# Output projections of two branches moved in between the pieces of a local attention group

## Chip, cores and metric

One Trainium2 chip, one of its cores. The time is the device time of one execution in microseconds; the kernel before has a median of 2757.5 us over 3 runs (2754.83 to 2759.94).

## What is computed

One decoder layer over 2048 tokens of width 1024, all in float32. Cut to what matters:

```python
h = x * (1 + scale) + shift
q, k, v, g_attn, u, B, C, g_conv, m_attn, m_conv = split(h @ W_in)
# A: three groups of 4 heads (dilation 1, 4, 16), each query sees 129 keys at its stride
o = sum_g(softmax_weight_g * attention_g(q, k, v))        # (2048, 512)
a_out = (o * silu(g_attn)) @ W_attn_out                   # 512 -> 1024
# B: gated short convolution
s_out = (B * conv3(C * u) * silu(g_conv)) @ W_conv_out    # 1024 -> 1024
merged = sigmoid(m_attn) * a_out + sigmoid(m_conv) * s_out
x = LayerNorm(alpha * x + (1 + gate) * (merged @ W_o))
```

## The kernel before, in words

Every float32 product is made of three products of float32r parts: each operand is split into a high part (a cast on ScalarE) and a low part (a subtraction on VectorE; the helper `split`, L465 to L467), and `mm3` (L563) or `pass3` (L119) adds high-high, high-low and low-high in PSUM. The instructions of all splits thus carry the lines L466 and L467.

The tile framework sets semaphores and the order of each engine's queue: it goes by the order of the program, lets ready instructions pass those that wait, and waits where a tile's buffer is not free. All loads and stores are issued by SyncE on one queue. Four stages follow one another.

1. The big projection h @ W_in, without v (L720 to L902). It works on blocks: `step` (L635) loads two 128-column blocks of weights, makes seven combinations of their quarters (`stationary_parts`, L536), and `products` (L578) forms seven block products over four rows of prepared `T` blocks, a Strassen-Winograd form with seven products in place of eight. Preparing one row of `T` (`t_row`, L513) takes seven splits and four subtractions, each of 128x512. `step` puts its products into the list `todo`, and they are traced in the next call, after the next weights have been prepared (`flush`, L621). Results go to DRAM scratch (q and k to `qk_scr`, the convolution branch to `y_scr`, the gates to `sg_scr` and `ga_scr`). During the first half `bias_tiles` (L704) turns the relative bias into tiles: it loads rows of `lagd` as overlapping windows, flips them with a product by `flip` (L714), copies and stores them. It is called for three groups, each right after a `step`, so before that step's products in program order.

2. Attention (`attention_stage`, L54). A list of segments `segs` holds the v products of 512-token quarters (pieces); `run_segs` (L94) walks it, loads weights up to 4 segments ahead, splits them up to 2 ahead, and runs pieces of attention hung behind the segments by `after`: scores and exponentials (`qk`), transposes (`tr`), weighted values (`pv`). First come the groups with dilation 4 and 16 for all quarters, called the dilated groups below, then the group with dilation 1, the local group (L352 to L418). Behind the local group's heads of each quarter `done` (L358) works out the softmax weights of the three groups through DRAM, and `merge` (L394) sums the three outputs and stores them in `om_scr`. The tile `o0` of each head has one buffer.

3. The output projections of the branches (L957 to L971). `co(0)`, then the attention branch over both halves, then `co(1)`: `step` and `products` again, over rows of `y_scr` (`load_y`) and `om_scr` (`load_o`). `gated` (L927) adds the last two block terms from PSUM (L940), multiplies by the gate (L941), and on the second branch adds the first one's result from `pa_scr` on GpSimd (L943). The sum goes to `mg_scr`, in blocks of 128 tokens.

4. The last projection and the norm (L974 to L1032). `load_w` scales the rows of W_o by the gate (L989); 8 steps over pairs of 128-token blocks from `mg_scr`; `norm` adds the residual (L1008, L1009), takes mean and variance with `bn_stats` and `bn_aggr` on VectorE (L1012 to L1016), scales on ScalarE (L1021), multiplies by g (L1022), adds b on GpSimd (L1023) and stores. `products_by_row` (L603) exists and is used for the first step of stage 1 alone: it runs all seven products of one row before the next row, with seven banks open.

```python
todo.append(lambda ...: (how or products)(S_, T, rows, *consumer()))   # L642, in step
```

## Time and profile before

| | |
|---|---|
| median of 3 runs | 2757.5 us |
| the profiled execution | 2760.77 us, span 2759.0 us, mean granted clock 0.944 |
| PE busy | 2478.2 us (90%) |
| DVE busy | 1821.2 us (66%) |
| ACT busy | 1059.2 us (38%) |
| POOL busy | 117.2 us (4%) |
| DMA | 364.03 MB, mean 132 GB/s |

PE is TensorE, DVE VectorE, ACT ScalarE, POOL GpSimd, SP SyncE. Busy time is a mean over the stages above. A granted clock of 1.00 is TensorE at 2.4 GHz, 0.50 at 1.2 GHz. The DMA share is the mean busy share of 16 DMA engines. Times in the rows are microseconds from the start of the span.

### The profile page before, as it was taken

Reading aid. Unit: us, or ns where it says so; the run is one execution under the profiler, and the core shown is the slowest. Engines: PE = TensorE matmul, PEld = TensorE weight load, DVE = VectorE, ACT = ScalarE, POOL = GpSimd, SP = SyncE. Lnnn points to the kernel's source line nnn. Section 1 sums busy time; section 2 is a strip of 40 time slices with the busy share of each in tenths; the row PEclk is TensorE's granted clock in tenths of the full one; section 3 lists DMA queues with packets and bytes.
Section 4 is the critical chain, followed back from the end, with each engine's and each line's share of the span. In section 5 each row is a group of like instructions: output and inputs, shape, how many; then the busy total and the mean of one; then the engine's idle time right before and its main releaser. Section 6 shows DMA issues by size and latency. Waiting matters only on the chain.

```text
span 2759.0 us, 31825 instructions
## 1 busy us (share of the span) xinstructions
PE 2478.2 (90%) x11734; PEld 2086.0 (76%) x11734; DVE 1821.2 (66%) x2996; ACT 1059.2 (38%) x1763; POOL 117.2 (4%) x78
## 2 busy tenths in 40 slices
PE   4998999999999999999999799999997358978886
PEld 2776788888877888888888599999986336656665
DVE  8753467667667555676655345544788787777987
ACT  5322333333344223333333355554653223243432
POOL 2000000000000000000000000000000000203123
PEclk8999999999999999999999899999998578989998
DMA  6333322213353333222222444534566655667343
GB/s 235 124 102 101 112 86 69 69 63 106 122 171 119 100 115 110 73 70 69 69 99 92 157 134 134 168 115 137 159 202 196 189 173 186 230 230 231 113 145 103
DMA packets 192265, 364.03 MB, mean 132 GB/s; under 512 B 20925, under 2 KB 91756, under 8 KB 192108
## 3 DMA queue, kind: packets, MB, share of 16 engines
q1 hardware_dynamic: 192108, 361.99, 40.7%
q8 instruction: 92, 1.51, 0.2%
q14 instruction: 65, 0.53, 0.1%
HBM read 268.03 MB, written 93.90 MB: 131 GB/s over the span
## 4 chain that ended last, share of the span: by engine, by line
PE 70%; DVE 11%; DMA 8%; issue 5%; ACT 3%; POOL 1%; SPq 1%; POOLq 0%; DVEq 0%; ACTq 0%
PE pb L566 19%; PE pb L567 19%; PE pb L568 19%; PE mm L123 3%; PE mm L121 3%; PE mm L122 3%; DVE tl L467 2%; DMA og<-o_scr 1%; PE pt L203 1%; DMA xs<-in_xn 1%; DMA ab<-al_scr 1%; DVE w2l L467 1%; DVE ab L407 1%; DMA raw<-mg_scr 1%; DVE o L408 0%
## 5 line engine op out<-in xcount | busy, mean ns | idle before, releaser
L566 PE MATMUL pb<-th,w2h 128*128 128x512 f32 x2304 | 918.6, 402 | 98.9 <-ACT th L466 74.0
L567 PE MATMUL pb<-tl,w2h 128*128 128x512 f32 x2304 | 916.2, 399 | 45.4 <-DVE tl L467 45.3
L568 PE MATMUL pb<-th,w2l 128*128 128x512 f32 x2304 | 907.9, 397 | 2.6 <-DVE w2l L467 2.6
L566 PEld LDWEIGHTS pb<-th,w2h 128*128 128x128 f32 x2304 | 441.8, 192 | 223.4 <-ACT th L466 96.0
L567 PEld LDWEIGHTS pb<-tl,w2h 128*128 128x128 f32 x2304 | 442.9, 192 | 148.3 <-DVE tl L467 57.4
L568 PEld LDWEIGHTS pb<-th,w2l 128*128 128x128 f32 x2304 | 442.9, 192 | 96.8 <-DVE w2l L467 4.9
L467 DVE TENSOR_TENSOR w2l<-raw,w2h 128x1024 fp32r<-128x1024 f32 (+1 forms) x192 | 237.8, 1239 | 166.2 <-ACT w2h L466 166.0
L466 ACT CAST w2h<-raw 128x1024 fp32r<-128x1024 f32 (+1 forms) x192 | 198.7, 1035 | 363.3 <-PE pb L567 348.4
L575 ACT COPY t<-pb 128x512 f32<-128x512 f32 x298 | 173.8, 584 | 412.8 <-PE pb L568 373.9
L121 PE MATMUL mm<-whi,hhi 128*128 128x256 f32 x768 | 253.4, 331 | 28.5 <-ACT hhi L466 28.4
L123 PE MATMUL mm<-whi,hlo 128*128 128x256 f32 x768 | 249.3, 327 | 3.4 <-DVE hlo L467 2.8
L122 PE MATMUL mm<-wlo,hhi 128*128 128x256 f32 x768 | 249.6, 326 | 1.9 <-DVE wlo L467 1.9
L121 PEld LDWEIGHTS mm<-whi,hhi 128*128 128x128 f32 x768 | 185.8, 242 | 32.2 <-ACT hhi L466 32.1
L123 PEld LDWEIGHTS mm<-whi,hlo 128*128 128x128 f32 x768 | 184.7, 242 | 5.5 <-DVE hlo L467 5.4
L122 PEld LDWEIGHTS mm<-wlo,hhi 128*128 128x128 f32 x768 | 186.1, 243 | 2.4 <-DVE wlo L467 2.3
L566 PE MATMUL pb<-th,w1h 128*128 128x512 f32 x384 | 154.2, 402 | 18.1 <-DVE big L1008 10.1
L466 ACT CAST w2h<-xs 128x1024 fp32r<-128x1024 f32 (+1 forms) x96 | 99.5, 1037 | 167.0 <-PE pb L567 141.1
L567 PE MATMUL pb<-tl,w1h 128*128 128x512 f32 x384 | 152.2, 396 | 0.0
L568 PE MATMUL pb<-th,w1l 128*128 128x512 f32 x384 | 151.8, 395 | 0.0
L943 POOL TENSOR_TENSOR big<-big,t 128x512 f32<-128x512 f32 x32 | 47.7, 1498 | 2437.2 <-DMA t<-pa_scr 2390.2
L466 ACT CAST w1h<-t 128x512 fp32r<-128x512 f32 (+1 forms) x96 | 58.8, 613 | 170.5 <-PE pb L567 163.1
L467 DVE TENSOR_TENSOR w2l<-xs,w2h 128x1024 fp32r<-128x1024 f32 (+1 forms) x96 | 116.1, 1210 | 11.5 <-ACT w2h L466 8.4
(161 smaller groups left out, 3072.7 us busy)
## 6 DMA issues: line engine op xcount, KB each, us to landing
raw<-in_w_main SPq DMA_DIRECT2D x152, 512.0 KB
qk_scr<-big SPq DMA_DIRECT2D x48, 512.0 KB
raw<-in_w_v SPq DMA_DIRECT2D x48, 512.0 KB
sg_scr<-big SPq DMA_DIRECT2D x32, 512.0 KB
big<-sg_scr SPq DMA_DIRECT2D x32, 512.0 KB
qr<-qk_scr SPq DMA_DIRECT2D x48, 256.0 KB
ab<-al_scr SPq DMA_DIRECT2D x48, 256.0 KB
kr<-qk_scr SPq DMA_DIRECT2D x36, 256.0 KB
```

The lines of the kernel that those rows point to most:

```text
L121: PE.matmul(o, a[0], b[0], start=start, stop=False)
L122: PE.matmul(o, a[0], b[1], start=False, stop=False)
L123: PE.matmul(o, a[1], b[0], start=False, stop=stop)
L203: PE.transpose(ps[:, n * P:(n + 1) * P], P_t[b][:, a:a + P], ident)
L407: V.tensor_mul(av, av, og)
L466: S.copy(hi, src)
L467: V.tensor_sub(lo, src, hi.bitcast(F32))
L566: PE.matmul(bank, a[0], b[0], start=start, stop=False, **kw)
L567: PE.matmul(bank, a[0], b[1], start=False, stop=False, **kw)
L568: PE.matmul(bank, a[1], b[0], start=False, stop=stop, **kw)
L575: S.copy(r, bank)
L943: G.tensor_add(o, o, a_)
```

## The change

Stage 3 is gone. In the attention stage each quarter of the local group is followed by 8 segments that project that quarter of the convolution branch (`co_segs`), and by 8 that project the quarter before of the attention branch (`ao_segs`); the last quarter's `ao_segs` come at the end. They are plain products with `pass3`, 24 (co) or 12 (ao) of 128x512 for each 128 output columns, gated by one multiplication from PSUM; the ao ones add co's result on VectorE. To make room, several tiles have fewer buffers. `bias_tiles` issues its loads at once and puts its flip products behind the step's products. The last projection's first step goes by rows, and its mean and variance come from two ScalarE passes with accumulated sums.

```diff
-        raw = wp.tile([P, DM], F32, name="raw", bufs=3)
+        raw = wp.tile([P, DM], F32, name="raw", bufs=2)
...
+    def parts_of(xs, store):
+        hi = hp.tile([P, CH], F32R, name="hhi", bufs=13)
+        lo = hp.tile([P, CH], F32R, name="hlo", bufs=13)
+        split(hi, lo, xs)
+        store.append((hi, lo))
...
-                hi = hp.tile([P, CH], F32R, name="hhi", bufs=9)
-                lo = hp.tile([P, CH], F32R, name="hlo", bufs=9)
...
+    def prep_rows(srcs, store):
+        def pre():
+            for src in srcs:
+                xs = hp.tile([P, CH], F32, name="xs", bufs=3)
+                SP.dma_start(xs, src)
+                parts_of(xs, store)
         return pre
...
+    def gemm(unit, rhs, base=0):
+        ps = bank("mm", 3)
+        for k, xk in enumerate(rhs):
+            sl = slice((base + k) * P, (base + k + 1) * P)
+            pass3(ps, [t[:, sl] for t in unit], xk, k == 0, k == len(rhs) - 1)
+        return ps
...
-        qr = kq.tile([P, CH], F32, name="qr", bufs=2)
-        kr = kq.tile([P, P + CH], F32, name="kr", bufs=2)
+        qr = kq.tile([P, CH], F32, name="qr", bufs=1)
+        kr = kq.tile([P, P + CH], F32, name="kr", bufs=1)
...
-                    pt = pa.tile([P, 256], F32, name="p", bufs=10)
+                    pt = pa.tile([P, 256], F32, name="p", bufs=8)
...
-                t = whole("ptf", transposed([(b, b) for b in range(4)]), slice(0, CH), 2)
+                t = whole("ptf", transposed([(b, b) for b in range(4)]), slice(0, CH), 1)
...
-            va = pa.tile([P, 3, 256], F32R, name="va", bufs=4)
-            vb = pa.tile([P, 3, 256], F32R, name="vb", bufs=4) if g < 2 else None
+            va = pa.tile([P, 3, 256], F32R, name="va", bufs=3)
+            vb = pa.tile([P, 3, 256], F32R, name="vb", bufs=3) if g < 2 else None
...
+    def co_segs(c):
+
+        ys, at = [], slice((c % 2) * CH, (c % 2 + 1) * CH)
+        for d in range(KT):
+            def coseg(i, unit, d=d):
+                sg = pm.tile([P, CH], F32, name="sg", bufs=2)
+                SP.dma_start(sg, sg_scr[c // 2, 1, d, :, at])
+                V.tensor_mul(sg, sg, gemm(unit, ys))
+                SP.dma_start(pa_scr[c // 2, d, :, at], sg)
+            seg([w_co[d]], coseg, prep_rows([y_scr[c // 2, k, :, at] for k in range(KT)], ys) if d == 0 else None)
+
+    def ao_segs(c):
+
+        os_, at, box = [], slice((c % 2) * CH, (c % 2 + 1) * CH), {}
+        for d in range(KT):
+            def aoseg(i, *units, d=d):
+                if units:
+                    box["u"] = units[0]
+                sg = pm.tile([P, CH], F32, name="sg", bufs=2)
+                co = pm.tile([P, CH], F32, name="co", bufs=2)
+                SP.dma_start(sg, sg_scr[c // 2, 0, d, :, at])
+                SP.dma_start(co, pa_scr[c // 2, d, :, at])
+                V.tensor_mul(sg, sg, gemm(box["u"], os_, base=(d % 2) * NH))
+                V.tensor_add(sg, sg, co)
+                SP.dma_start(mg_scr[c * 4:(c + 1) * 4, :, d, :].rearrange("b q t -> q b t"),
+                             sg.rearrange("q (b t) -> q b t", t=P))
+            seg([w_ao[d // 2]] if d % 2 == 0 else [], aoseg,
+                prep_rows([om_scr[c, :, j, :] for j in range(NH)], os_) if d == 0 else None)
...
-                ab = pm.tile([P, CH], F32, name="ab", bufs=4)
+                ab = pm.tile([P, CH], F32, name="ab", bufs=3)
...
-            gt = pm.tile([P, CH], F32, name="gt", bufs=2)
+            gt = pm.tile([P, CH], F32, name="gt", bufs=1)
...
         pre_all(first, xn[c], h, None)
+        co_segs(c)
+        if c > 0:
+            ao_segs(c - 1)
+    ao_segs(NCH - 1)
...
-        w = 256 if g < 2 else P
+        w, hks = 256 if g < 2 else P, []
         for j0 in range(0, NH, 2):
-            hk, r = half(), half()
+            hk = half()
+            hks.append(hk)
...
+        def tiles():
+            for j0, hk in zip(range(0, NH, 2), hks):
+                r, pf = half(), ps_bank()
...
+        return tiles
...
-                    bias_tiles((W_Q, W_Q + 2, W_K).index(u), flips[0])
+                    todo.append(bias_tiles((W_Q, W_Q + 2, W_K).index(u), flips[0]))
...
-    def load_o(p, i):
...
-    def gated(which, p, d, last):
...
-    co(0, False)
...
-    co(1, True)
...
-                    sts = w.tile([P, 2, 6], F32, name="bns", bufs=2)
-                    for h2 in range(2):
-                        V.bn_stats(sts[:, h2], z[:, h2 * CH:(h2 + 1) * CH])
...
+                    mv = w.tile([P, 4], F32, name="mv", bufs=2)
+                    o = raw_tile()
+                    S.activation(o, z, AF.Copy, scale=-1.0 / DM, accum_out=mv[:, 0:1])
+                    S.activation(o, z, AF.Square, bias=mv[:, 0:1], accum_out=mv[:, 1:2])
+                    V.tensor_scalar(mv[:, 1:2], mv[:, 1:2], 1.0 / DM, LN_EPS, op0=ALU.mult, op1=ALU.add)
+                    G.tensor_tensor(mv[:, 2:3], mv[:, 1:2], powe, op=ALU.pow)
+                    V.tensor_mul(mv[:, 3:4], mv[:, 0:1], mv[:, 2:3])
+                    S.activation(z, z, AF.Identity, scale=mv[:, 2:3], bias=mv[:, 3:4])
...
-             CH, [(T, range(4), norm)], pre)
+             CH, [(T, range(4), norm)], pre, products_by_row if tb == 0 else None)
```

## Rows read from the trace of the kernel before

**Rows 1.** The page, part 1: busy time of each engine.

```profile
PE 2478.2 (90%) x11734; PEld 2086.0 (76%) x11734; DVE 1821.2 (66%) x2996; ACT 1059.2 (38%) x1763; POOL 117.2 (4%) x78
```

**Rows 2.** Windows: busy us (instructions) of PE, PEld, DVE, ACT, POOL; clock, DMA share, GB/s.

```profile
414.00:483.00 69.00, 69.00 (x306) 57.15 (x305) 50.00 (x63) 23.82 (x30) 0.00 (x0) 1.00 0.21 69
...
1575.00:1980.00 405.00, 398.62 (x2572) 394.04 (x2570) 214.24 (x548) 213.80 (x503) 0.00 (x0) 0.99 0.50 146
...
1980.00:2240.00 260.00, 157.18 (x1064) 148.47 (x1065) 214.09 (x461) 101.95 (x247) 0.00 (x0) 0.75 0.63 189
2240.00:2543.00 303.00, 259.55 (x1011) 193.12 (x1009) 233.26 (x345) 105.37 (x169) 47.37 (x32) 0.92 0.63 212
1980.00:2543.00 563.00, 416.73 (x2073) 341.59 (x2073) 447.36 (x805) 207.32 (x416) 47.37 (x32) 0.84 0.63 201
...
2580.00:2741.00 161.00, 143.06 (x593) 114.28 (x591) 131.85 (x195) 51.81 (x62) 46.72 (x28) 0.95 0.39 132
```

**Rows 3.** Shorter windows of the same kind, 10 and 20 us long.

```profile
10.00:20.00 10.00, 0.00 (x0) 0.00 (x0) 9.83 (x33) 3.18 (x4) 0.00 (x0) 1.00 0.89 324
...
1680.00:1700.00 20.00, 20.00 (x173) 19.99 (x172) 15.69 (x36) 12.51 (x31) 0.00 (x0) 1.00 0.66 196
...
2060.00:2080.00 20.00, 14.20 (x63) 12.51 (x64) 16.41 (x27) 7.12 (x13) 0.00 (x0) 0.59 0.78 260
...
2160.00:2180.00 20.00, 4.26 (x17) 3.56 (x17) 15.07 (x21) 0.96 (x2) 0.00 (x0) 0.50 0.76 221
```

**Rows 4.** Waits of PE, 1980 to 2240: us in total, times, longest.

```profile
PE ot L121 <- DVE o L360: 34.0, 7, 17.2
```

**Rows 5.** Groups of instructions: count, busy us, mean ns, idle before and its releasers.

```profile
L467 DVE TENSOR_TENSOR tl<-big,th 128x512 fp32r<-128x512 f32 x96 | 63.9, 685 | 5.4 <-ACT th L466 5.3
...
L467 DVE TENSOR_TENSOR wlo<-raw,whi 128x1024 fp32r<-128x1024 f32 x48 | 58.5, 1220 | 66.6 <-ACT whi L466 66.4
...
L943 POOL TENSOR_TENSOR big<-big,t 128x512 f32<-128x512 f32 x32 | 47.7, 1498 | 2437.2 <-DMA t<-pa_scr 2390.2 <-DVE big L941 30.7 <-issue 8.4
L941 DVE TENSOR_TENSOR big<-big,t 128x512 f32<-128x512 f32 x64 | 46.0, 738 | 1.5 <-issue 1.1
...
L940 DVE TENSOR_TENSOR t<-t,pb 128x512 f32<-128x512 f32 x64 | 42.9, 683 | 22.9 <-ACT t L575 11.1 <-PE pb L568 6.4 <-POOL big L943 5.2
```

**Rows 6.** DMA issues: transfer, queue, count, size of one.

```profile
raw<-in_w_co SPq DMA_DIRECT2D x16, 512.0 KB
...
raw<-in_w_ao SPq DMA_DIRECT2D x4, 512.0 KB
```

**Rows 7.** Timelines of SP and ACT: start, us, line, instruction.

```profile
1624.95 0.33 SPq L143 DMA_DIRECT2D qr<-qk_scr  x1
...
1638.48 1.14 ACT L149 ACTIVATE qh<-qr 128x512 f32<-128x512 f32 x1 [0.77 <-PE s L122]
```

**Rows 8.** The chain that ended last: start, us, a 256 KB load.

```profile
2070.40 6.51 DMA xs<-in_xn
```

**Rows 9.** PE at the flip products: its waits from 150 to 420, and a window.

```profile
PE pb L714 <- DMA t<-lagd: 14.2, 3, 6.1
...
220.00:230.00 10.00, 4.13 (x10) 3.34 (x11) 1.20 (x2) 1.05 (x4) 0.00 (x0) 0.66 0.42 129
```

**Rows 10.** Last projection: three groups, PE waits 2580 to 2741, timelines.

```profile
L1014 DVE BATCH_NORM_STATS2 bns<-big 128x6 f32<-128x512 f32 x32 | 21.4, 677 | 0.1
...
L1021 ACT ACTIVATE big<-big,rs 128x1024 f32<-128x1024 f32 x16 | 19.9, 1244 | 42.3 <-DVE rs L1020 42.3
...
L672 ACT ACTIVATION_READ_ACCUMULATOR wt<-wt 128x1 f32 x24 | 4.5, 186 | 0.0
...
PE pb L566 <- DVE big L1008: 10.1, 4, 4.3
...
2577.07 0.68 DVE L467 TENSOR_TENSOR tl<-big,th 128x512 fp32r<-128x512 f32 x1
...
2593.62 0.39 PE L568 MATMUL pb<-th,w1l 128*128 128x512 f32 x1
```

More of the change, by code (lines that the diff above doesn't have):

```diff
@@ L51, in bucket_rows, with attention_stage @@
     return oh
-def attention_stage(tc, psum1, wp, hp, kq, pa, pm, split, ident, scp, mod, w_v, xm, xn,
-                    qk_scr, nb_scr, ga_scr, o_scr, st_scr, st0_scr, al_scr, om_scr):
+def attention_stage(tc, psum1, wp, hp, kq, pa, pm, split, ident, scp, mod, w_v, w_ao, w_co, xm, xn,
+                    qk_scr, nb_scr, ga_scr, o_scr, st_scr, st0_scr, al_scr, om_scr, y_scr, sg_scr, pa_scr, mg_scr):
     nc = tc.nc
@@ L78, in pre @@
                 V.tensor_scalar(xs, xs, scp[:, k:k + 1], mod[:, 0, k:k + 1], op0=ALU.mult, op1=ALU.add)
[L79 to L82 removed]
+                parts_of(xs, store)
+        return pre
+    def prep_rows(srcs, store):
[3 more added lines that the diff above has]
+                SP.dma_start(xs, src)
+                parts_of(xs, store)
         return pre
@@ L129, in classes_of @@
         return t.rearrange("p (a r) -> p r a", r=4)
-    nb = [[kq.tile([P, 256 if g < 2 else P], F32, name=f"nb{g}{j}") for j in range(NH)]
-          for g in range(3)]
+    nb = [[kq.tile([P, P if g == 2 else 256], F32, name=f"nb{g % 2}{j}" if g < 2 else f"nb{g}{j}")
+           for j in range(NH)] for g in range(3)]
     def load_nb(g):
@@ L229, in tr @@
             PT[2] = [t[:, :256] for t in parts(ps, 256)]
-            t = whole("ptf", ps, slice(256, 384 + len(edge) * P), 2)
+            t = whole("ptf", ps, slice(256, 384 + len(edge) * P), 1)
             PT[3] = t[:, :P]
@@ L909, in layer_kernel @@
         wp, hp, kq, pa, pm = (pool(n) for n in ("wp", "hp", "kq", "pa", "pm"))
-        attention_stage(tc, psum1, wp, hp, kq, pa, pm, split, ident, scp, mod, w_v, xm, xn,
-                        qk_scr, nb_scr, ga_scr, o_scr, st_scr, st0_scr, al_scr, om_scr)
-    def load_o(p, i):
-        def load(xa, xb):
-            for t, j in ((xa, i), (xb, i + 2)):
-                for cc in range(2):
-                    SP.dma_start(t[:, cc * CH:(cc + 1) * CH], om_scr[2 * p + cc, :, j, :])
-        return load
@@ L921, in load_y @@
-    def load_y(p, i):
-        def load(xa, xb):
-            for t, k in ((xa, i), (xb, i + 4)):
-                SP.dma_start(t[:, :PAIR], y_scr[p, k])
-        return load
-    def gated(which, p, d, last):
-        def consumer():
-            m = [big()[:, :PAIR] for _ in range(2)]
-            for k in range(2):
-                SP.dma_start(m[k], sg_scr[p, which, d + k])
-            def put(k, at):
-                def f(r, bank):
-                    t, o = half(), m[k][:, at:at + CH]
-                    if last:
-                        a_ = half()
-                        SP.dma_start(a_, pa_scr[p, d + k, :, at:at + CH])
-                    V.tensor_add(t, r, bank)
-                    V.tensor_mul(o, o, t)
-                    if last:
-                        G.tensor_add(o, o, a_)
-                    if (k, at) in ((0, CH), (1, 0)):
-                        if last:
-                            SP.dma_start(mg_scr[p * 8:(p + 1) * 8, :, d + k, :].rearrange("b q t -> q b t"),
-                                         m[k].rearrange("q (b t) -> q b t", t=P))
-                        else:
-                            SP.dma_start(pa_scr[p, d + k], m[k])
-                return f
-            return put(0, 0), put(0, CH), put(1, 0), put(1, CH)
-        return consumer
@@ L955, in layer_kernel @@
-    w = ctx.enter_context(block_products())
-    def co(p, last):
-        T = {}
-        pre = t_rows(T, [(i, load_y(p, i)) for i in range(4)])
-        for d in range(0, KT, 2):
-            step(w, w_co[d], w_co[d + 1], CH, [(T, range(4), gated(1, p, d, last))], pre)
-            pre = None
-    co(0, False)
-    T = {}
-    pre = t_rows(T, [(2 * p + i, load_o(p, i)) for p in range(2) for i in range(2)])
-    for d in range(0, KT, 2):
-        step(w, w_ao[d // 2], None, 256,
-             [(T, range(2 * p, 2 * p + 2), gated(0, p, d, p == 0)) for p in range(2)], pre)
-        pre = None
@@ L971, in layer_kernel @@
-    co(1, True)
+        attention_stage(tc, psum1, wp, hp, kq, pa, pm, split, ident, scp, mod, w_v, w_ao, w_co, xm, xn,
+                        qk_scr, nb_scr, ga_scr, o_scr, st_scr, st0_scr, al_scr, om_scr, y_scr, sg_scr, pa_scr, mg_scr)
+    w = ctx.enter_context(block_products())
     T, rows_ = {}, {}
```

20 lines of the change are left out of this document (5 added, 15 removed).

## The prediction

> **What bounds the kernel now.** I read the page's busy line first, then the windows by stage, then 20 us windows inside the stages that the diff touches, then groups, waits and timelines there. PE is busy 90% of the span [rows 1], but that is a mean over unlike stages [rows 2]. In the big projection PE never stops: 306 products in 69 us, 0.2255 us per 512-column product, at full clock. In the dilated groups it is busy 399 of 405 us. In the local group (1980 to 2240) it is busy 157 of 260 us at a mean granted clock of 0.75, so it sits at the 1.2 GHz level about half the time, while DVE works 214 us. Inside that stage [rows 3], 2160 to 2180 has 4 us of PE and 15 of DVE: V products are done, and what is left is the chain of weights, merge and store. The longest PE wait, 34.0 us, is for the merge to free the output tile [rows 4]. In the output projections (2240 to 2543) the roles turn: PE 260 of 303 us. DMA has a share of 0.63 in both. So one stage starves PE, the next feeds it, and nothing overlaps them.
>
> **Part 1: projections into the local stage.** I cost the stretch 1980 to 2543, 563 us, by engine.
>
> PE: removed 1008 products of 512 columns (co twice 4 steps x 7 x 4 x 3, ao 4 x 2 x 7 x 2 x 3), added 4 quarters x (8 x 8 x 3 + 8 x 4 x 3) = 1152. At 0.2255 that is 260 us. The local group's own 1064 instructions (almost all 256 columns or fewer) ran at 173 per 20 us in a full-clock window [rows 3], so 1064 x 0.116 = 123 us. Together 383 us.
>
> DVE, with the mean durations of [rows 5]: removed 12 row preparations x 11 operations x 0.685 = 90 us, 8 wide weight preparations x 7.2 (three 1024-wide splits at 1.22, five half-width operations at about 0.7) = 57, 4 half-width ones x 4 = 16, 64 gated outputs x (0.683 + 0.738) = 91; sum 254. Added: 48 input splits x 0.685 = 33, 48 weight splits x 1.22 = 59, 32 single gatings x 0.68 = 22, 32 gating-and-sums x 1.42 = 45; sum 159. 447 - 254 + 159 = 352 us. POOL's 32 sums (47.7 us) become DVE's, already counted. ACT falls too (fewer splits, no product copies) from 207 us; it binds nowhere.
>
> DMA: the stretch moved 563 x 201 GB/s = 113 MB at share 0.63, or 355 us of all 16 engines, 319 GB/s per full share. w_co is loaded four times instead of twice (32 loads of 512 KB for 16), w_ao 16 times for 4 [rows 6]: +14.7 MB. Some 4 MB of it belongs to the last projection. So 124 MB, 389 us of full share.
>
> Three resources at 383, 352 and 389 us is the crux. What share can be held? The best 10 us windows reach 0.89, and 2060 to 2080 held 0.78 [rows 3]. Plain quarters also demand unevenly: a co slice moves 1.28 MB in 5.4 us of PE, an ao slice 1.15 MB in 2.7 us, so ao slices wait for DMA (1.15 MB / 284 GB/s = 4.05 us) and the local attention (13.2 MB, 46 us) does as well. Per quarter 46 + 8 x 5.43 + 8 x 4.05 = 122 us without smoothing, 115 with it. The first quarter's V products precede 1980, so some 60 to 70 us remain of it, then three quarters of 115 to 122, then 32 for the last ao: 437 to 468 us. I take **460**, a share of 0.85: **-103 us**. Ends: 408 (PE at 94%, where the dilated groups hold 98%) and 617 (share stays at the 0.63 seen).
>
> What is moved past a queue: the SP queue issues 256 transfers of this kind instead of 148, about 0.33 us each [rows 7], +36 us spread over 460; only where it blocks does it matter. Each slice's store (pa or mg) waits on SP for its gating, with the next weight and gate loads behind it; two raw buffers give one slice of cover (5.4 us) against a 6.5 us load seen on the chain of waits [rows 8]. That is inside the 460 as DMA-paced slices.
>
> The Trainium skill, DMA: Bandwidth & Descriptors, section "Measured (HBM→SBUF, 128 partitions, SWDGE, issued from GpSimd)", asks for batches of 1 MiB and speaks against cutting y, sg and pa from 512 to 256 KB. Window 2060 to 2080, mostly 256 KB transfers, shows 260 GB/s at share 0.78, no worse per share than the stretch. Taking its 138 GB/s for 64 KB pieces as a floor, an estimate, the stage would last 124 / 0.138 = 900 us; no row here is near that, and I give it no chance of its own.
>
> **Part 2: bias tiles later.** Now the flip products stand on PE right behind their loads: three waits of 14.2 us in all; 220 to 230 holds the longest and shows a clock of 0.66 [rows 9], so some products after each wait run at the lower level, which I put at 2 us in all. Deferred behind a step of 84 products (19 us), loads have landed. The flip products themselves stay. Ends 0 and 17, I take **-15**. Without that cover the 14.2 us come back.
>
> **Part 3: last projection.** By rows: preparation of w_o ends on DVE at 2577.8, but the first step's last product starts at 2593.6 [rows 10], because each product needs all four rows. By rows, only the last row's 21 products (4.7 us) follow: up to 12 us; eight additions at the end and seven of eight banks held cost some back: **-7** (0 to -12). Statistics: DVE loses 16 x (2 x 0.677 + 0.1) = 23 us; in 2580 to 2741 it is busy 132 of 161 us and PE waits 10.1 us for its output adds, of 18 us of PE gaps [rows 2, 10]. ACT gains 16 x 2 x (1.24 + 0.19) = 46 us on 52 in 161, covered. **-8** (0 to -18). The tail after the last product gets longer: two ACT passes and reads (2.9) for two DVE passes (1.4), and two row blocks share ACT: **+2** (1 to 6). Junk outputs take raw buffers that the next load could use; those loads have been split before, so nothing. Sum **-13**.
>
> **Part 4: fewer buffers** also govern the dilated groups. qr is loaded at 1624.95 and cast at 1638.48 [rows 7]: 13.5 us of slack against 6.5 for a load, so one buffer does: 0, end +20 for all of them together.
>
> Sum: the profiled execution is 2760.8 us (span 2759.0); 2760.8 - 103 - 15 - 13 = 2629.8. It stands 3.3 above the median of 2757.5, so I forecast **2626 us**.
>
> **Rivals.**
>
> *PE-paced (0.13).* DMA loads smooth out over quarters and the stage runs almost like the dilated groups, PE at 94%: 383 / 0.94 = 408. 2626 - 52 = 2574. For: the dilated groups' 399 of 405 us, in the same queue order [rows 2]. Against: 389 us in 408 is a share of 0.95, above anything seen.
>
> *Half the overlap (0.14).* Share 0.72, as in bursts of the old stages: 540 us, 2706. The same number covers the change not doing what it says: if the issue order puts the slices behind the last attention piece instead of between, only parts 2 and 3 are left, 2729.
>
> *Slower: the single SP queue (0.08).* Every store waits in order for its gating, with loads behind it; if this keeps DMA at the 0.63 of before, 617 us, +54: 2626 + 157 = 2783. It decides at a share of 389 / (563 + 28) = 0.66. For: both old stages, with their own waits, never averaged more. Against: there the idle share came from the merge chain and from four-row preparations, which the change removes or covers.
>
> *Bubbles in the dilated groups (0.05).* Single buffers make each of 32 heads wait. A shown load of 6.5 us, half of it exposed, costs 104 us: 2730; only above 4.1 us per head would the whole gain go. Against: the 13.5 us slack. The Trainium skill, Perfetto Trace Analysis, section "Identifying the Most-Contended Engine", reads a regular bubble on the engine that should be full as too little SBUF for the next tile; no run here shows it yet.
>
> **How the numbers follow.** The forecast case has 0.60. A measurement of this kernel tells some 0.2% (5.5 us) from no change. Slower holds the SP rival without its edge, 0.07; between it and the half overlap 0.02 falls within 0.2%; the rest, 0.91, is faster. Range: down to the PE-paced case, 2574; up past the half overlap and most of the undone overlap, 2715; beyond lie the SP rival and the worst bubbles, and the slack below 2574.
>
> **What would show it.** Right: no stretch after 1980 with PE under half busy until the last projection; PE near 0.83 and DMA near 0.85 in a stage of about 460 us at full clock; lagd waits gone between 210 and 290; the last stage near 203 us, no bn rows, and its first step ending within 8 us of the w_o preparation. Wrong: DMA share below 0.7 with PE waiting on weight or gate loads (SP rival); products of 512 columns only after the last V product (no interleaving); new PE waits for qh, va or ptf between 1575 and 1980 (bubbles).

## The result, and the profile after

The changed kernel takes **2719.7 us** (median of 4 runs, 2715.2 to 2724.8). The kernel before, run beside it on the same chip, takes 2758.7 (4 runs, 2754.8 to 2762.2). The ratio is 0.9859, with a 95% interval of 0.9837 to 0.9882: faster by 39 us, or 1.4%. The forecast was 2626 with a range of 2574 to 2715. So the direction was right and the size was not: the gain is under a third of what was forecast, and the time lies above the range.

The profiled execution of the changed kernel has a span of 2713.4 us against 2759.0 before, 45.6 less. Lines are renumbered in the changed kernel: the three products of a piece in the attention stage are now L139 to L141, in the steps of the projections L617 to L619; splits are L517 (ACT) and L518 (DVE), the co slices L318 to L320, the ao slices L332 to L336, the merge L446 to L459, the load of a step's weights L680, and the last projection L986 to L1020.

The page's busy line for PE (busy us, share, instructions) answers to [rows 1]:

```profile
PE 2482.0 (91%) x11878; PEld 2102.1 (77%) x11878; DVE 1721.0 (63%) x2787; ACT 1057.3 (39%) x1741; POOL 74.1 (3%) x46
```

PE's share has hardly moved, DVE lost 100 us, and POOL lost its 32 sums. As before, the total says little. The stages are told apart best by two groups of stores: the last one of the dilated groups (into o_scr), and the last one of the gated products (into mg_scr). First the kernel before (duration in ns min/median/max, then first and last start in us):

```profile
L323 SPq DMA_DIRECT2D o_scr<-o x32: 364/376/387, 1622.4 to 1983.1; - x32
...
L946 SPq DMA_DIRECT2D mg_scr<-big x16: 370/371/371, 2364.6 to 2543.3; - x16
```

and the same two tensors in the changed kernel:

```profile
L370 SPq DMA_DIRECT2D o_scr<-o x32: 370/371/432, 1599.0 to 1949.8; - x32
...
L336 SPq DMA_DIRECT2D mg_scr<-sg x32: 370/371/472, 2128.7 to 2461.5; - x32
```

| stretch of the profiled execution | before | after | change | forecast |
|---|---|---|---|---|
| to the first dilated store | 1622.4 | 1599.0 | -23.4 | -15 |
| dilated groups | 360.7 | 350.8 | -9.9 | 0 |
| combined stage, to the last mg store | 560.2 | 511.7 | -48.5 | -103 |
| last stage, to the end | 215.7 | 251.9 | +36.2 | -13 |
| sum | 2759.0 | 2713.4 | -45.6 | -131 |

So two terms failed, by 54.5 and 49.2 us, and two came out better, by 8.4 and 9.9. The windows of the changed kernel, with the columns of [rows 2] (busy us and instructions of PE, PEld, DVE, ACT, POOL; clock, DMA share, GB/s), show each stretch:

```profile
210.00:290.00 80.00, 80.00 (x359) 66.54 (x358) 39.52 (x48) 25.12 (x41) 0.00 (x0) 1.00 0.42 138
...
1575.00:1980.00 405.00, 404.36 (x2602) 399.84 (x2602) 221.83 (x573) 214.89 (x520) 0.00 (x0) 1.00 0.50 145
...
1950.00:2461.00 511.00, 420.99 (x2230) 360.73 (x2230) 347.59 (x626) 166.29 (x322) 0.00 (x0) 0.92 0.77 244
...
2342.00:2352.00 10.00, 10.00 (x53) 8.52 (x52) 3.52 (x6) 2.10 (x2) 0.00 (x0) 1.00 0.34 110
...
2382.00:2392.00 10.00, 0.00 (x0) 0.00 (x0) 6.07 (x8) 0.00 (x0) 0.00 (x0) 0.50 0.89 276
...
2461.00:2713.00 252.00, 185.52 (x672) 137.57 (x672) 176.54 (x231) 111.69 (x161) 57.84 (x32) 0.85 0.36 118
```

**Combined stage.** It moved 511 x 244 GB/s = 124.7 MB, where 124 were forecast, and DVE worked 348 us, where 352 were forecast. The share is 0.77 in the place of 0.85, and PE was busy for 421 us, not 383. Its granted clock averaged 0.92 (383 / 0.92 = 416, an estimate, since that mean counts PE's idle time too). Behind a long wait products of 512 columns run at the 1.2 GHz level: after 18.3 us of waiting they start 0.43 us apart for some 5 us (granted clock 0.50 from 2394 to 2399), before they go back to 0.23 (1.00 from 2400 to 2402):

```profile
2393.78 0.80 PE L139 MATMUL mm<-hhi,whi 128*128 128x512 f32 x1 [18.33 <-DVE sg L334]
2394.38 0.63 PE L140 MATMUL mm<-hlo,whi 128*128 128x512 f32 x1
2394.80 0.63 PE L141 MATMUL mm<-hhi,wlo 128*128 128x512 f32 x1
...
2400.52 0.39 PE L140 MATMUL mm<-hlo,whi 128*128 128x512 f32 x1
2400.75 0.39 PE L141 MATMUL mm<-hhi,wlo 128*128 128x512 f32 x1
```

In the last quarter the two resources take turns: PE is full at a DMA share of 0.34 in 2342 to 2352, and PE stands still at 0.89 in 2382 to 2392. PE's longest waits from 1950 to 2480 (us in total, times, longest) are these:

```profile
PE mm L139 <- DVE sg L334: 46.5, 14, 18.3
PE pt L221 <- ACT p L214: 25.0, 5, 9.7
PE pb L617 <- ACT th L517: 16.2, 2, 15.8
```

The first is a product bank that the gating has not yet emptied. What the gating itself waits for stands in the group of that line, over 1950 to 2465 (count, busy us, mean ns, idle before it and its releaser):

```profile
L334 DVE TENSOR_TENSOR sg<-sg,mm 128x512 f32<-128x512 f32 x32 | 21.9, 686 | 39.6 <-DMA sg<-sg_scr 39.3
```

The gate's load is late. It takes one of two sg tiles, and SP's waits over the same time show it standing until the store of such a tile has landed:

```profile
SPq L332 <- DMA mg_scr<-sg: 20.8, 20, 2.3
```

That is not all that holds the loads. SP itself, the one queue, waits for 303 of the 511 us (all its waits added up), most of all with a store whose sum (L336) or gating (L320) is not done:

```profile
SPq L336 <- DVE sg L335: 43.8, 23, 3.4
SPq L320 <- DVE sg L319: 37.5, 20, 5.5
```

**Last stage.** It forms the same products (672 instructions of PE before and after), 36 us slower. SP's waits there, 2465 to 2713, in the changed kernel:

```profile
SPq L1020 <- POOL big L1019: 111.6, 16, 10.9
SPq L680 <- ACT raw L1013: 41.4, 6, 9.8
```

The second row is new. L1013 is the Square pass, L680 the load of the next step's weights. The pass writes its discarded output into a raw tile, and there are three of these; each load of weights that turns to it waits on SP until ACT has finished. Behind that load stand the loads of x and the stores.

### The profile page after: what moved, and what is told of

It reads as the page before. It is cut to its first block, busy times and chain, and to the rows that moved or that the text cites. A ratio compares the mean times of both kernels' runs of the same rounds, so it can differ in the third digit from the quotient of the medians.

```text
span 2713.4 us, 32007 instructions
## 1 busy us (share of the span) xinstructions
PE 2482.0 (91%) x11878; PEld 2102.1 (77%) x11878; DVE 1721.0 (63%) x2787; ACT 1057.3 (39%) x1741; POOL 74.1 (3%) x46
## 4 chain that ended last, share of the span: by engine, by line
PE 70%; DMA 11%; DVE 9%; issue 6%; ACT 2%; POOL 1%; SPq 1%; POOLq 0%; DVEq 0%; ACTq 0%
PE pb L617 17%; PE pb L619 17%; PE pb L618 17%; PE mm L139 5%; PE mm L140 5%; PE mm L141 5%; DMA sg<-sg_scr 2%; DVE tl L518 1%; DMA ab<-al_scr 1%; DMA og<-o_scr 1%; DMA mg_scr<-sg 1%; DMA xs<-in_xn 1%; PE pt L221 1%; POOL big L1019 1%; DMA kr<-qk_scr 1%
## 5 line engine op out<-in xcount | busy, mean ns | idle before, releaser
L617 PE MATMUL pb<-th,w2h 128*128 128x512 f32 x2016 | 800.0, 399 | 84.0 <-ACT th L517 58.6
L618 PE MATMUL pb<-tl,w2h 128*128 128x512 f32 x2016 | 799.3, 397 | 9.9 <-DVE tl L518 9.8
L619 PE MATMUL pb<-th,w2l 128*128 128x512 f32 x2016 | 797.1, 397 | 12.0 <-DVE w2l L518 12.0
L617 PEld LDWEIGHTS pb<-th,w2h 128*128 128x128 f32 x2016 | 385.7, 191 | 180.6 <-ACT th L517 68.1
L619 PEld LDWEIGHTS pb<-th,w2l 128*128 128x128 f32 x2016 | 386.8, 192 | 96.1 <-DVE w2l L518 16.0
L517 ACT CAST w2h<-raw 128x1024 fp32r<-128x1024 f32 x168 | 176.7, 1052 | 345.6 <-PE pb L618 285.9
L518 DVE TENSOR_TENSOR w2l<-raw,w2h 128x1024 fp32r<-128x1024 f32 x168 | 214.2, 1275 | 150.0 <-ACT w2h L517 149.8
L139 PE MATMUL mm<-whi,hhi 128*128 128x256 f32 x768 | 250.6, 327 | 19.4 <-ACT hhi L517 15.9
L141 PE MATMUL mm<-whi,hlo 128*128 128x256 f32 x768 | 247.2, 324 | 2.6 <-DVE hlo L518 2.6
L139 PEld LDWEIGHTS mm<-whi,hhi 128*128 128x128 f32 x768 | 184.9, 241 | 21.3 <-ACT hhi L517 17.4
L139 PE MATMUL mm<-hhi,whi 128*128 128x512 f32 x384 | 158.4, 413 | 45.4 <-DVE sg L334 43.1
L141 PEld LDWEIGHTS mm<-whi,hlo 128*128 128x128 f32 x768 | 184.1, 241 | 3.2 <-DVE hlo L518 3.2
L517 ACT CAST whi<-raw 128x1024 fp32r<-128x1024 f32 x96 | 100.6, 1048 | 168.9 <-PE mm L140 70.9
L518 DVE TENSOR_TENSOR wlo<-raw,whi 128x1024 fp32r<-128x1024 f32 x96 | 116.9, 1219 | 69.8 <-ACT whi L517 69.5
L140 PE MATMUL mm<-hlo,whi 128*128 128x512 f32 x384 | 155.4, 405 | 0.2 <-DVE hlo L518 0.2
L141 PE MATMUL mm<-hhi,wlo 128*128 128x512 f32 x384 | 155.3, 405 | 0.0
L517 ACT CAST w2h<-xs 128x1024 fp32r<-128x1024 f32 x84 | 88.6, 1055 | 132.8 <-PE pb L618 114.4
L617 PE MATMUL pb<-th,w1h 128*128 128x512 f32 x336 | 132.6, 395 | 3.5 <-DVE big L1006 3.0
```

Source lines behind the costliest of these rows:

```text
L139: PE.matmul(o, a[0], b[0], start=start, stop=False)
L140: PE.matmul(o, a[0], b[1], start=False, stop=False)
L141: PE.matmul(o, a[1], b[0], start=False, stop=stop)
L517: S.copy(hi, src)
L518: V.tensor_sub(lo, src, hi.bitcast(F32))
L617: PE.matmul(bank, a[0], b[0], start=start, stop=False, **kw)
```

## The experiments

All times are medians of four runs; ratios are against the kernel before, run beside them. The last mg store of each profile splits its span, so that the stages can be read alone.

**The last projection: four runs.** The first puts the old statistics on VectorE back, the second gives the discarded output a tile of its own (and narrows the padding of big, which pays for it), the third undoes the by-rows opening, and the fourth puts ScalarE's statistics alone into the kernel before.

The edit of s1 (that of s4 is the same one the other way round, in the kernel before, with the raw tile):

```diff
...
-                    o = raw_tile()
-                    S.activation(o, z, AF.Copy, scale=-1.0 / DM, accum_out=mv[:, 0:1])
-                    S.activation(o, z, AF.Square, bias=mv[:, 0:1], accum_out=mv[:, 1:2])
...
+                    for h2 in range(2):
+                        V.bn_stats(sts[:, h2], z[:, h2 * CH:(h2 + 1) * CH])
+                    mv = w.tile([P, 2], F32, name="mv", bufs=2)
+                    V.bn_aggr(mv, sts)
...
```

Of s2:

```diff
-        return rooms["work"].tile([P, PAIR + 64], F32, name="big", bufs=4)
+        return rooms["work"].tile([P, PAIR + 16], F32, name="big", bufs=4)
...
-                    o = raw_tile()
+                    o = w.tile([P, DM], F32, name="junk")
```

Of s3:

```diff
-             CH, [(T, range(4), norm)], pre, products_by_row if tb == 0 else None)
+             CH, [(T, range(4), norm)], pre)
```

> The changed kernel with the old statistics (bn_stats and bn_aggr on VectorE) in the last projection, all else as changed. Last stage of the changed kernel: 252 us from the last mg store to the end, against 216 before. Theory A (the statistics' discarded output takes a raw buffer, so the next weights load late): the last stage falls to about 205, the whole to 2672 us (2660 to 2685). Theory B (the two ScalarE passes themselves sit in front of ScalarE's casts and copies): the same, 2672. Theory C (opening by rows is what costs): stays at 2710 or above.

> The changed kernel with the discarded output of the two ScalarE passes in a tile of its own instead of a raw tile (room made by 192 bytes less padding of each big tile). Theory A: raw loads no longer wait for the Square pass (41 us of such waits now), a step falls from 26.9 us to about 20, the whole to 2675 us (2660 to 2690). Theory B: steps stay above 25 us, the whole at 2705 or above. Theory C: no change either.

> The changed kernel with its last projection opened product by product as before. Theories A and B: slower by what opening by rows saves, 5 to 12 us: 2725 to 2732 us. Theory C: faster by 20 us or more, below 2700.

> The kernel before with the new ScalarE statistics alone. Theories A and B: slower by 35 to 48 us, about 2800 us (2790 to 2807). Theory C: within 10 us of before, 2750 to 2768 us. My prediction's step would have it faster, 2752.

| kernel | time | ratio and interval | last stage |
|---|---|---|---|
| changed | 2719.7 | 0.9859 [0.9837, 0.9882] | 251.9 |
| s1 statistics on VectorE | 2692.6 | 0.9751 [0.9733, 0.9769] | 223.8 |
| s2 tile of its own | 2688.6 | 0.9733 [0.9717, 0.9750] | 220.3 |
| s3 without by rows | 2727.8 | 0.9878 [0.9858, 0.9897] | 258.0 |
| s4 before, statistics on ScalarE | 2794.9 | 1.0120 [1.0105, 1.0136] | 245.9 |

One tile of 4 KB per partition is worth 31 us, and s2 still does both passes on ScalarE: so it is not the passes that cost the time, but the buffer in which their output sat. (The narrower padding was not run alone, but s1 comes to nearly the same time without it.) s4 agrees from the other side: the statistics alone make the kernel before 1.2% slower, with 30 us more in its last stage (215.7 to 245.9). In s2 SP's waits, 2469 to 2685, no longer name the pass:

```profile
SPq L1020 <- POOL big L1019: 98.2, 16, 12.3
SPq L680 <- DVE w2l L518: 28.2, 6, 8.4
SPq L680 <- DVE t L610: 19.6, 4, 9.8
```

The loads now wait for the splits that read the raw tiles, as they did in the kernel before. The distance from the first store of the output to the last shows the same thing without any attribution. In the changed kernel:

```profile
L1020 SPq DMA_DIRECT2D out_y<-big x16: 337/338/344, 2523.6 to 2709.9; - x16
```

That is 186.3 us; in s2

```profile
L1020 SPq DMA_DIRECT2D out_y<-big x16: 337/344/344, 2530.2 to 2681.7; - x16
```

it is 151.5, and 151.5 also in the kernel before. The two others with the output in a raw tile have 186.9 (s3) and 185.5 (s4), and s1 has 154.3. The row of the kernel before:

```profile
L1024 SPq DMA_DIRECT2D out_y<-big x16: 337/343/344, 2603.8 to 2755.3; - x16
```

Without the buffer's cost, ScalarE's statistics save 3.5 us of the last stage against s1 (220.3 for 223.8); the intervals of the two times overlap, so it is not settled that they save anything. Taking by rows away costs 8 us by the medians and 6 in the stage, but the intervals overlap here too.

**The bias tiles alone.** The kernel before with that one edit (the flip products of a pair of heads go into the list of deferred work).

```diff
...
-                    bias_tiles((W_Q, W_Q + 2, W_K).index(u), flips[0])
+                    todo.append(bias_tiles((W_Q, W_Q + 2, W_K).index(u), flips[0]))
```

> The kernel before with the bias tiles' products deferred as in the change and nothing else. The prediction's part 2: 15 us faster (0 to 17), 2744 against 2759. Theory A: exactly that, the waits for the lagd loads between 210 and 290 gone and all later work 15 us earlier. Rival: the attention of the changed kernel starts 25 us earlier, so the deferral is worth 22 to 25 us by itself, 2735; otherwise some 10 us of these come from the buffers or from another part.

2741.7 us, ratio 0.9929 (0.9906 to 0.9951): 18 us faster, and by the profile the dilated groups' first and last stores come 21 us sooner (1601.3 and 1961.8). The attention's first product starts at 1573.4 before, at 1553.7 in s8 and at 1548.5 in the changed kernel: of the 25 us in the rival, 20 are the bias tiles', and no run takes the other 5 apart. The window of the kernel before and that of s8 say why it is more than 15. Before:

```profile
210.00:290.00 80.00, 65.78 (x265) 53.31 (x264) 27.69 (x33) 19.41 (x32) 0.00 (x0) 0.89 0.35 112
```

and s8:

```profile
210.00:290.00 80.00, 80.00 (x359) 66.57 (x358) 39.16 (x48) 25.60 (x40) 0.00 (x0) 1.00 0.42 138
```

In the same 80 us PE does 94 more products, at 0.2255 us 21.2 us of work: 14.2 us of waits, and by this estimate 7 us for products that ran at the lower clock behind them.

**What paces the combined stage: the gate buffers.** Three or four sg and co tiles instead of two, paid for with hhi and hlo; then the sum written into the co tile and stored from there, so that sg is free sooner at no memory.

The edit of s5 (s6 has 11 for 12 and 4 for 3; hlo as hhi, and sg alike in the co slices):

```diff
-        hi = hp.tile([P, CH], F32R, name="hhi", bufs=13)
+        hi = hp.tile([P, CH], F32R, name="hhi", bufs=12)
...
-                sg = pm.tile([P, CH], F32, name="sg", bufs=2)
-                co = pm.tile([P, CH], F32, name="co", bufs=2)
+                sg = pm.tile([P, CH], F32, name="sg", bufs=3)
+                co = pm.tile([P, CH], F32, name="co", bufs=3)
```

Of s7:

```diff
-                V.tensor_add(sg, sg, co)
+                V.tensor_add(co, sg, co)
...
-                             sg.rearrange("q (b t) -> q b t", t=P))
+                             co.rearrange("q (b t) -> q b t", t=P))
```

> The changed kernel with three buffers instead of two for the gate tile sg and the co tile of the output slices (and twelve instead of thirteen of hhi and hlo, which pay for the memory). Theory A, an ao slice lasts as long as the round trip of its two gate buffers (load, gating, store landed, load again): the last eight ao slices run some 4 us apart in the place of 4.5, the waits of the PE products for sg's gating (46.5 us between 1980 and 2465) fall by a third, time 10 to 20 us under the changed kernel's 2719.7, 2700 to 2710. Theory B, the transfers' bandwidth paces the slices: same time within 4 us and the same DMA share near 0.79. Theory C, the merge's operations stand ahead of the slices on SP and DVE (the 18.3 us wait around 2375): that one wait stays, 0 to 5 us gained.

> The changed kernel with four buffers for sg and co (eleven of hhi and hlo). Theory A (round trip of the buffers): a further 5 to 15 us below the kernel with three, 2690 to 2705. Theory B (bandwidth): same as the changed kernel within 4 us. Theory C (merges ahead in the queue): 0 to 8 us, the long wait around 2375 stays; if the fewer hhi and hlo matter, 1575 to 1980 shows PE waits for hhi that the changed kernel has not.

> The changed kernel with the sum written into the co tile and stored from there, so that a gate buffer is free once the sum has read it, without any more memory; the co tile then carries the wait for the store. Theory A (round trip of the gate buffer): half of what three buffers give, 5 to 10 us, 2710 to 2715. Theory B: no change, 2716 to 2724. Theory C: no change but for 0 to 3 us.

2710.3 (ratio 0.9814, 0.9789 to 0.9839), 2701.9 (0.9780, 0.9753 to 0.9807) and 2714.1 (0.9829, 0.9806 to 0.9851). The round trip of two tiles is part of the pace: the combined stage takes 498.7 and 498.9 us in s5 and s6, for 511.7, so by the profiles the third tile does it. But s6's profiled execution is the slowest of its four (2712.1), so a fourth tile may be worth more than its profile shows. Only s6's interval lies clear of the changed kernel's. s7's gain of 6 us does not, so storing from the co tile remains unproven, though its profile, of its fastest run, has the combined stage at 502.7. What they are paid with cannot be told from the scatter: the dilated groups take 354.7 and 352.8 us with twelve and eleven hhi, and 350.7 to 353.9 in the profiles with thirteen. In the combined stage PE waits 19.4 (s5) and 21.0 us (s6) for hhi, against 0.3 in the changed kernel, but 10.4 in s9 with thirteen; whether the payment causes this was not tried.

**The merges.** First they are spread over every second slice; then they get back the buffers that the change took from them.

Of s9:

```diff
-            after(len(segs) + 3 + jj, lambda jj=jj, merge=merge: merge(jj))
+            after(len(segs) + 3 + 2 * jj, lambda jj=jj, merge=merge: merge(jj))
```

Of s10 (hhi and hlo as in s5):

```diff
-                ab = pm.tile([P, CH], F32, name="ab", bufs=3)
+                ab = pm.tile([P, CH], F32, name="ab", bufs=4)
...
-            gt = pm.tile([P, CH], F32, name="gt", bufs=1)
+            gt = pm.tile([P, CH], F32, name="gt", bufs=2)
```

> The changed kernel with the four merges of a quarter behind every second slice (the 4th, 6th, 8th and 10th) instead of behind four slices in a row. Nothing else, no more memory. Theory C (the merges' loads and stores stand in a block ahead of the slices' own on SP, and their operations on DVE): the wait of 18.3 us around 2375 goes, and smaller ones in the quarters before; 10 to 20 us faster than the changed kernel, 2700 to 2710. Theory B (bandwidth of the transfers paces the stage): no change within 5 us, because the same bytes only come in another order. Rival of its own: the last ao slices get the merges' work into their midst, the stage ends as late or up to 5 us later.

> The changed kernel with the merge's buffers as they were before (four ab, two gt), paid for by twelve hhi and hlo instead of thirteen. The prediction costed the fewer buffers at 0, with an end of +20. Theory: the merges run one after the other because ab and gt have too few buffers, so the 18.3 us wait around 2375 falls to about 10 and the time by 5 to 10 us, to 2710 to 2715. Rival: each merge waits for its og loads, whose two buffers are as before; no change within 5 us, or up to 5 us slower through the hhi.

2714.9 (0.9830, 0.9807 to 0.9853) and 2728.0 (0.9881, 0.9861 to 0.9901). In the changed kernel the block of merges is plain on SP around the 18.3 us wait (start, us, line, transfer):

```profile
2384.99 0.32 SPq L446 DMA_DIRECT2D ab<-al_scr  x1
2385.72 0.32 SPq L459 DMA_DIRECT2D om_scr<-o  x1
2386.13 0.38 SPq L452 DMA_DIRECT2D og<-o_scr  x1
2386.57 0.62 SPq L457 DMA_DIRECT2D gt<-ga_scr  x1
2387.24 0.49 SPq L320 DMA_DIRECT2D pa_scr<-sg  x1
2387.78 0.43 SPq L332 DMA_DIRECT2D sg<-sg_scr  x1
```

The pa store at 2387.24 had its data ready at 2371.3 (its gating started on DVE at 2370.63) and stood behind the merges' loads for 16 us, with the first ao gate load behind it. Yet undoing the block moves the wait (12.5 us long in s9) and brings 5 us, within what the intervals leave open. More merge buffers bring nothing: the combined stage of s10 takes 522.3 us, 11 more, with one wait of 20.2 us for a co slice's gating. Whether the twelve hhi or the merges' earlier loads do that is not settled; s5 has the twelve hhi too, and its stage is shorter.

**The two repairs together**, and the two with spread merges:

> The changed kernel with the discarded output in a tile of its own and four gate and co buffers. If the two repairs touch different stages, their gains add: 31 us of the first and some 18 of the second below the changed kernel's 2719.7, so 2670. If the end of the output slices only moves the wait to the opening of the last projection, whose weights then load no sooner, the second gain is lost: 2685.

> Both repairs and the merges behind every second slice. If the three add, 2655 to 2662; if buffers and spread merges cure the same waits (the PE products waiting for sg's gating), no better than the two alone, 2668 to 2672.

s11 takes 2675.0 (0.9692, 0.9676 to 0.9708): the gains of s2 and s6 add to within 4 us. s12 takes 2682.3 (0.9719, 0.9701 to 0.9736), so spreading the merges is no gain where there are four gate tiles.

**Which resource paces what is left.** On s11, s13 leaves out a third of the slices' products, s14 leaves out the loads of the co half, and s15 moves the sums from DVE to POOL.

Of s13, in the products of both kinds of slices:

```diff
-            pass3(ps, [t[:, sl] for t in unit], xk, k == 0, k == len(rhs) - 1)
+            PE.matmul(ps, unit[0][:, sl], xk[0], start=k == 0, stop=False)
+            PE.matmul(ps, unit[1][:, sl], xk[0], start=False, stop=k == len(rhs) - 1)
```

Of s14:

```diff
-                SP.dma_start(co, pa_scr[c // 2, d, :, at])
...
-                V.tensor_add(sg, sg, co)
+                V.tensor_add(sg, sg, sg)
```

Of s15:

```diff
-                V.tensor_add(sg, sg, co)
+                G.tensor_add(sg, sg, co)
```

> The kernel with both repairs (2675.0) with two of the three products of each piece in the output slices: it leaves out the products of the high part of the weights with the low part of the input, 384 products of 512 columns. At 0.2255 us they are 87 us at full clock. Theory P, PE paces the stage (busy 425 of 488 us): 70 to 87 us faster, 2588 to 2605. Theory B, the transfers pace it: 0 to 15 us faster, 2660 to 2675, and the DMA share of the stage stays near 0.79. A mixture, in which slices wait for transfers and attention pieces for PE: in between, near 2630, with a lower clock.

> The kernel with both repairs (2675.0) without the loads of the co half into the ao slices; it leaves out the sum with the co half (sg is added to itself, so DVE does the same work). 32 transfers of 256 KB, 8.4 MB, fewer; at 315 GB/s per full share they are 27 us. Theory B, bandwidth paces the stage: 20 to 27 us faster, 2648 to 2655. Theory P: 0 to 6 us faster. Round trip of buffers: the gate load that comes before it on the same queue lands sooner, 5 to 10 us faster.

> The kernel with both repairs (2675.0) with the ao slices' sums on POOL, as they were before the change. DVE loses 32 operations of 0.69 us, 22 us of its 342 in the stage; POOL's take some 1.5 us each, and DVE's beside them may take longer, as the splits of the last projection do (2.68 us for 1.22). Theory D, DVE's order holds the banks back: 10 to 20 us faster, 2655 to 2665. Theories P and B: no change, or up to 10 us slower through the longer chain from product to store and the operations beside POOL's.

| kernel | time | ratio and interval | combined stage |
|---|---|---|---|
| s11 | 2675.0 | 0.9692 [0.9676, 0.9708] | 492.4 |
| s13 two products | 2658.6 | 0.9641 [0.9624, 0.9658] | 477.7 |
| s14 no co load | 2649.2 | 0.9612 [0.9596, 0.9628] | 464.3 |
| s15 sums on POOL | 2684.8 | 0.9734 [0.9718, 0.9749] | 504.7 |

87 us of products are worth 16; 27 us of transfers are worth 26, their full price. The window of the stage in s13

```profile
1955.00:2425.00 470.00, 335.47 (x1832) 288.48 (x1832) 343.55 (x623) 163.71 (x321) 0.00 (x0) 0.85 0.82 259
```

has PE at 335 of 470 us, its clock down to 0.85 and the DMA share up to 0.82, beside s11's

```profile
1955.00:2448.00 493.00, 428.69 (x2233) 364.24 (x2231) 346.18 (x629) 167.23 (x325) 0.00 (x0) 0.92 0.79 252
```

and in s14

```profile
1955.00:2420.00 465.00, 417.32 (x2224) 356.71 (x2224) 345.10 (x626) 167.04 (x322) 0.00 (x0) 0.95 0.78 248
```

the share stays and the stage shrinks with the bytes. PE is busiest, but it is not the engine to relieve. What paces lies on the side of the transfers, whose share is 0.77 to 0.82 in these versions. That it is their bytes is not shown: s14 also takes 32 issues off SP and shortens each ao slice's chain, so its 26 us need not be bandwidth alone. SP's waits still add up to 284 of the 493 us in s11, and no run took stores off its queue, so that rival is open. s15 is slower by 10: POOL's sums take 1.46 us each for 0.69, and SP's waits with an mg store for its sum grow from 35.3 to 50.1 us (L336), with the next gate load behind them.

**Uneven demand as the cause of the low share.** In the last quarter alone, co and ao slices in turn (on s2; then with three gate and co tiles and twelve hhi and hlo).

```diff
+        at = len(segs)
         co_segs(c)
         if c > 0:
             ao_segs(c - 1)
+        if c == NCH - 1:
+            segs[at:] = [s for two in zip(segs[at:at + KT], segs[at + KT:]) for s in two]
```

> The changed kernel with the discarded output in a tile of its own (2688.6 by itself) and, in the last quarter alone, the co slices of that quarter and the ao slices of the quarter before in turn instead of one set after the other. Theory, uneven demand over time lowers the share: PE's work of a pair (5.4 + 2.7 us) stands beside 2.43 MB (7.7 us at 315 GB/s), so the stretch loses some 10 us of the idle transfers in front and of the PE waits behind: 2674 to 2682. Rival, the merges in front of the ao slices and the two gate buffers pace the tail in whatever order: 2685 to 2692.

> The same with three gate and co buffers and twelve hhi and hlo. Theory: the order and the buffers cure the same waits in part; 5 to 10 us below s16 where both matter, 2668 to 2675, which would be the fastest of all. Rival: no better than the four buffers in the old order, 2675 or above.

s16 takes 2690.5 (0.9745, 0.9721 to 0.9769), the time of s2: the theory missed. s17 takes 2671.4 (0.9689, 0.9670 to 0.9708), the lowest of the kernels that compute everything, though not to be told from s11. From 2330 to 2450 the windows of s2

```profile
2330.00:2450.00 120.00, 90.57 (x393) 72.86 (x392) 65.33 (x100) 18.38 (x28) 0.00 (x0) 0.87 0.70 213
```

and s16

```profile
2330.00:2450.00 120.00, 91.33 (x403) 74.11 (x403) 68.72 (x108) 18.98 (x29) 0.00 (x0) 0.87 0.70 214
```

are alike in every column, where s17

```profile
2330.00:2450.00 120.00, 93.64 (x409) 75.45 (x406) 72.71 (x112) 21.66 (x33) 0.00 (x0) 0.88 0.78 245
```

moves 15% more in the same time. In the old order three gate tiles (s5) and four (s11) have

```profile
2330.00:2450.00 120.00, 97.19 (x437) 78.98 (x435) 71.12 (x111) 21.32 (x33) 0.00 (x0) 0.90 0.73 231
...
2330.00:2450.00 120.00, 96.73 (x416) 76.87 (x415) 70.41 (x110) 21.09 (x32) 0.00 (x0) 0.90 0.76 241
```

So more gate tiles raise the share there in whatever order. With two tiles the order does nothing. With three, 245 GB/s in turn stand against 231 in the old order, so it may then be worth something; s5 lacks the tile for the discarded output, and no run has only the order between it and s17.

## Why the prediction was right and wrong

**Part 3 failed in one sentence.** "Junk outputs take raw buffers that the next load could use; those loads have been split before, so nothing." The raw tiles had been split, but a tile that a ScalarE pass writes is taken until the pass is done, and the pass comes only when both halves of its row block are summed. Three tiles served two loads per step; with two discarded outputs per step as well, the load of the next step's weights waited for the end of the present one (41.4 us of SP's waits), and the cover of the load was gone. The price was 31 us (s2), and 36 of the 49 us by which the last stage missed its forecast can be told from runs: these 31, and some 5 because the statistics were put at -8 and are worth -3.5 at most. Of the rest, 7 us are a cover that the forecast did not see go. Before, w_o was prepared from 2524.8 on, 18.5 us ahead of the last mg store, under the last co step, and was ready 34.5 us behind it [rows 10]. Now the loads start at 2458.9, 2.6 us ahead, among the last mg stores on SP, and the preparation ends 41 us behind the last of these; PE waits 15.8 us for its first piece. The last 6 us have not been taken apart.

**By rows: the mechanism is right.** The w_o preparation now ends at 2502.8 on DVE (2577.8 before), and the first step's last product starts at 2503.24 at the latest, 0.4 us later, where it was 16 [rows 10] and "within 8" was the sign given. The changed kernel's timelines show it: DVE's last split of the preparation and its first of the second step's weights, then PE's last product of the first step, and the first that waits for those weights:

```profile
2502.16 0.68 DVE L518 TENSOR_TENSOR tl<-t,th 128x512 fp32r<-128x512 f32 x1
2502.76 1.22 DVE L518 TENSOR_TENSOR w2l<-raw,w2h 128x1024 fp32r<-128x1024 f32 x1
...
2503.24 0.40 PE L619 MATMUL pb<-th,w2l 128*128 128x512 f32 x1
2504.03 0.50 PE L619 MATMUL pb<-th,w2l 128*128 128x512 f32 x1 [0.40 <-DVE w2l L518]
```

Undone, it costs 6 to 8 us against the 7 forecast, with overlapping intervals, so the runs don't settle that it saves anything.

**Part 2: the mechanism is right, the size too small.** -15 was given, with 0 and 17 as ends; 18 to 21 were measured, above the upper end. The mis-sized term is the 2 us put on products at the lower level behind the waits: by the estimate from s8 they are 7.

**Part 1: the resources were counted rightly, the share was not.** Bytes (124.7 MB for 124) and DVE (348 us for 352) were right; PE's 383 us became 421, at a mean clock of 0.92. Two steps failed. The first is the sentence "That is inside the 460 as DMA-paced slices": two raw tiles were looked at for cover, and the two gate tiles, whose load waits for a store, were not. More of them are worth 13 us in the changed kernel and 20 beside s2 (512.1 to 492.4). The second is the larger, "I take 460, a share of 0.85". The remaining 35 us to the 457 that the forecast makes of this stretch are the way from that share to the 0.79 of s11: 124.2 MB at the 319 GB/s per full share of the forecast are 389 us, and 389 / 0.79 = 493. This restates the measured share and does not explain it. The row for 0.85 should have been a mean over a stretch with waits, not the best 10 us windows [rows 3]. Why no version holds more than 0.82 is open: with two gate tiles the order of the slices (s16) is not the answer, spreading the merges (s9) moved no more than the intervals leave open, PE's work (s13) is a small part of it, and the single queue was not tried. Of the rivals, the half overlap (share 0.72, 540 us) came nearer to this stage than the forecast's 0.85; its total of 2706 missed too, mainly because it took Part 3's 13 us as given.

**Part 4: right for what it looked at.** Fewer merge buffers cost nothing that s10 could show, and no bubbles came into the dilated groups: PE is busy 404 of 405 us there. What the forecast did not price is the buffers that grew, thirteen hhi and hlo for nine. The groups take 9.9 us less; PE waited 5.0 us for hhi there before (8 waits from 1575 to 1980) and never does now. That this is the whole cause was not tried. The Trainium skill, Perfetto Trace Analysis, section "Optimization Strategy" (the prediction names the section before it), says that a gap that repeats on the engine that should be full can mean too little memory for the next tile. Where the gap came, in the ao slices, s5 and s6 agree (13 us of the stage for a third gate tile), and the merges' tiles in s10 do not (no gain).

**SP queue rival.** It needed a share of 0.63, and the time it forecast did not come true. Its mechanism is there: stores hold loads behind them, as in the 16 us above, and SP waits for 303 of the 511 us. How much of the missing share that is, no run tells. The Trainium skill, DMA: Bandwidth & Descriptors, section "Measured (HBM→SBUF, 128 partitions, SWDGE, issued from GpSimd)", asks for batches of 1 MiB and has 138 GB/s for 64 KB. The runs here, with pieces of 256 and 512 KB, stay well above that row: the stage moved 244 GB/s, and with four gate tiles 252.

## What to carry to other kernels

A discarded output is a tile like any other: before giving it a buffer of a pool that loads use, ask which load takes that buffer next, and when the writing pass runs. When three resources are each costed near the length of a stage, forecast with the mean share that a stretch with such waits has held, and follow each tile that is loaded, worked on and stored again through its whole round trip: with more such tiles the transfers reached more here. When a stage is folded into another, the one after it can lose the cover that it had (7 us here).

## What was not expected

The engine with the highest busy share (428.7 of 493 us) was not the one to relieve: 87 us of its work, at full clock, gave 16. Its mean clock fell from 0.92 to 0.85 with that, yet the slices' products that were left did not get dearer (412 ns on average for 417, L134 in s13 and L139 in s11); PE simply waited longer for the gating (72.4 us for 20.2 at these lines). And moving 32 sums from DVE (346 us busy in that stage) to an idle POOL made the kernel 10 us slower: each sum stands in the chain from a gate's load to its store.
